# One float32 transpose, one matmul pass, in turn: re-ordering TensorE in the attention stages of a two-block transformer kernel

## The chip, the core and the metric

The kernel runs on one core of a Trainium2 chip. The metric is device time in microseconds (us) of one execution, taken as the median of several runs. TensorE is called PE in the profile; its weight loads have a row of their own (PEld) because a load can run beside the matmul before it. VectorE is DVE, ScalarE is ACT, GpSimd is POOL, and SP issues most of the DMAs.

## What is computed

Two transformer blocks on 512 tokens of width 1024, in float32. The change touches only the attention part of the first block:

```python
q = rmsnorm(q_m.reshape(bsz, s, MEM_HEADS, MEM_HEAD_DIM), memq_gain)   # 4 heads of 128
k = rmsnorm(k_m.reshape(bsz, m, MEM_HEADS, MEM_HEAD_DIM), memk_gain)   # 256 memory rows
p = softmax(q @ k.T * 128 ** -0.5);  y_mem = p @ v                     # memory attention
y_moba = moba_attention(qh, kh, vh)   # 8 heads of 64, causal over blocks of 256 keys;
                                      # with 512 tokens both blocks are always selected
merged = (sigmoid(g1 + bg1) * (y_conv @ w_br_conv) + sigmoid(g2 + bg2) * (y_moba @ w_br_moba)
          + sigmoid(g3 + bg3) * (y_mem @ w_br_mem))
```

Everything after that (the projection, two feed-forward layers, the second block) is matrix products and is not touched.

## The kernel before

**Products.** A float32 product is made of three passes over operands that were split into a high and a low part (`split`, L214 to L221): high by high, high by low, low by high. One pass is one matmul of 128 stationary by 512 moving columns. `gemm_t_steps` (L229, passes at L237 to L239) accumulates one output tile in one PSUM bank over eight k; `gemm_n_steps` (L242, passes at L249 to L251) runs four banks side by side. Both are generators: one step is three passes. `W.take` streams the weights in chunks of 128x1024: SP loads a chunk, ACT makes its high part (L96), DVE its low part (L97).

**Attention as a strand, products as filler.** `mem_head` (L521) is one head of the memory attention, `moba_pair` (L586) two heads of the block attention. Each is a strand of small PE work with long waits on ACT and DVE in between: transposes, scores, softmax, transposes of the probabilities, the product with v. `in_turns` (L265) writes a strand and, at each of its yields, as many steps of a filler as the yield says: the q, k, v projections behind the memory heads, the products of the convolution branch behind the block attention. The numbers come from `PACE_M` and `PACE_B`. Before the heads, the products for q of the memory attention (`qm_steps`) carry the transposes of k of the memory (`transpose_km`, two groups of four, both written at k = 4).

**Transposes.** A transpose is a float32 matmul of one 128x128 tile with the tile as stationary operand and an identity as moving operand, so each brings its own weight load. They come in groups of two to four into one PSUM bank. Most groups use the pool `ps_t`, which has a single bank: the next group can start only when ACT (L217) and DVE (L218) have both read the last one. In `moba_pair` the inner loop runs j = 0, 1, 2 for each of two heads: transposes (L643, L650), the split of the bank into a high part on ACT and a low part on DVE, then `PACE_B[5]` steps of filler, then the products with v (L660, L663; tile `oa`). In the first two rounds of the first head, one score product of the second head and `PACE_B[6]` steps follow the filler.

**Order.** The program order is not the order on the engines: at build time a scheduler of the framework places the instructions by its own estimate of when their inputs are ready. `as_written` (L141) takes this freedom away for the engines it names: each instruction traced inside it is tied to the one before it on its engine. In the kernel before, it holds for SP, ACT and DVE from the start to L482 and in the last stage, and nowhere for PE. Accumulating passes into one bank keep their order in any case.

Of the kernel before, what the change touches and what calls it, by code (L numbers as in the profile page):

```python
# [15 lines left out]
P = 128  # L16
S = 512
M = 256
# [12 lines left out]
FILL = (4, 8)  # L31

ORDER = (2, 3, 1, 0)

PACE_M = (5, 2, 6, 5, 5)
PACE_B = (4, 2, 2, 2, 3, 2, 1)


VECS = [
# [72 lines left out]
def build(ctx: ExitStack, tc: tile.TileContext, a: dict, out: bass.AP, dbg=None):  # L112
    nc = tc.nc
# [113 lines left out]
    def bank(p=None, tag="acc", name="acc"):  # L227
        return (p or acc).tile([P, 512], F32, tag=tag, name=name)
# [3 lines left out]
    def gemm_t_steps(ps, ops, name, row0, col):  # L232

        n = len(ops)
        for k, (ah, al) in enumerate(ops):
            wh, wl = W.take(name, row0 + k * P, col)
            mm(ps, lhsT=wh, rhs=ah, start=(k == 0), stop=False)  # L237
            mm(ps, lhsT=wh, rhs=al, start=False, stop=False)  # L238
            mm(ps, lhsT=wl, rhs=ah, start=False, stop=(k == n - 1))  # L239
            yield  # L240

    def gemm_n_steps(pss, ops, name, col):  # L242

        n = len(ops)
        for k, (ah, al) in enumerate(ops):
            wh, wl = W.take(name, k * P, col, 512)
            for i, ps in enumerate(pss):
                t = slice(i * P, (i + 1) * P)
                mm(ps, lhsT=ah[:, t], rhs=wh, start=(k == 0), stop=False)  # L249
                mm(ps, lhsT=ah[:, t], rhs=wl, start=False, stop=False)  # L250
                mm(ps, lhsT=al[:, t], rhs=wh, start=False, stop=(k == n - 1))  # L251
                yield

# [10 lines left out]
    def in_turns(strand, filler):  # L264

        for n in strand:
            for _ in range(n):
                next(filler, None)

    def rsqrt(sums, n, inv, name):  # L270

# [169 lines left out]

    pq = [bank() for _ in range(4)]
    qm_steps = gemm_n_steps(pq, h, "w_in", 3072)
    for _ in range(4):
        next(qm_steps)
    km_raw = [yp.tile([P, 512], F32, tag=f"kmr{i}", name=f"kmr{i}") for i in range(2)]
    normed_rows([(km_raw[i], pk[i]) for i in range(2)], 4, "km", rmem)
# [2 lines left out]
    nc.vector.tensor_scalar(qg[:, 1:2], V("memq_gain"), 128 ** -0.5, None, ALU.mult)  # L450
    kmT = [pair(yp, f"kmT{i}", f"kmT{i}", 1, 2 * M) for i in range(2)]

    def transpose_km():
        for g in range(2):
            pt = bank(ps_t, "pt", "kmt")
            for hh in range(2):
                for i in range(2):
                    c = (2 * g + hh) * P
                    nc.tensor.transpose(pt[:, hh * M + i * P: hh * M + (i + 1) * P], km_raw[i][:, c:c + P], ident)
            split(*kmT[g], pt, V("memk_gain"))  # L460


    for k in range(KT):
        if k == FILL[0]:
            transpose_km()
        if k >= 4:
            row_sums(ssx, k - 4)
        if k:
            for _ in range(4):
                next(qm_steps)  # L470
        if k == 0:
            for i in range(2):
                split(*vm[i], pk[2 + i], rmem[:, i:i + 1])
        elif k == 1:
            for i in range(2):
                load_rows("x", i)
        elif k == 2:
            for i in range(2, 4):
                load_rows("x", i)
        if k + 3 < KT:  # L480
            make_h(k + 3)
# [38 lines left out]

    def mem_head(hd):  # L521
        pt = bank(ps_t, "pt", "qmt")
        for i in range(4):
            nc.tensor.transpose(pt[:, i * P:(i + 1) * P], qm_raw[i][:, hd * P:(hd + 1) * P], ident)
        qT = pair(yp, "qmT", f"qmT{hd}", 1)
        split(*qT, pt, qg[:, 1:2])
        yield PACE_M[0]
# [14 lines left out]
        po = bank(ps_o, "po", "om")  # L542
        for kt in range(2):
            pt = bank(ps_t, "pt", "pmt")
            for i in range(4):
                nc.tensor.transpose(pt[:, i * P:(i + 1) * P], probs[i // 2][:, i % 2, kt * P:(kt + 1) * P], ident)
            ph, pl = pair(yp, "pmT", f"pmT{hd}_{kt}", 2)
            split(ph, pl, pt)
            yield PACE_M[3 + kt]
            vh, vl = (x[:, hd * P:(hd + 1) * P] for x in vm[kt])  # L550
            mm(po, lhsT=vh, rhs=ph, start=(kt == 0), stop=False)
            mm(po, lhsT=vh, rhs=pl, start=False, stop=False)
            mm(po, lhsT=vl, rhs=ph, start=False, stop=(kt == 1))
        split(*y_mem[hd], po)

    filler = qkv_steps()
    for _ in range(FILL[1]):
        next(filler)
    for hd in range(4):
        in_turns(mem_head(hd), filler)  # L560
# [25 lines left out]
    def moba_pair(g):  # L586

        c = slice(g * P, (g + 1) * P)
        pt = bank(name="qt")
        for i in range(4):  # L590
            nc.tensor.transpose(pt[:, i * P:(i + 1) * P], q_raw[i][:, c], ident)

        qq = [at.tile([P, S], F32R, tag=f"qq{s_}", name=f"qq{g}{s_}") for s_ in range(2)]
        for s_ in range(2):
# [2 lines left out]
            nc.vector.scalar_tensor_tensor(qq[s_][e, :], pt[d, :], qg[d, 0:1], qq[s_][d, :].bitcast(F32),  # L597
                                           op0=ALU.mult, op1=ALU.subtract)
        pt = bank(ps_s, "ps", "kt")
        for i in range(4):  # L600
            nc.tensor.transpose(pt[:, i * P:(i + 1) * P], k_raw[i][:, c], ident)
        for s_ in range(2):
            d, e = slice(64 * s_, 64 * s_ + 64), slice(64 - 64 * s_, P - 64 * s_)
            split(kk[d, s_, :], kz[d, s_, :], pt[d, :], V("moba_k_gain")[d, :])
# [31 lines left out]
        for s_ in range(2):  # L636
# [2 lines left out]
            fl = dict(skip_group_check=True)  # L639
            for j in range(3):  # L640
                pt = bank(ps_t, "pt", "pat")
                for i in range(j, 4):
                    nc.tensor.transpose(pt[:, i * P:(i + 1) * P], probs[s_][i][:, j * P:(j + 1) * P], ident)  # L643
                if j < 2:
                    c0, o = j * P, j * P
                    ph, pl = pair(at, f"pT{j}", f"pT{g}{s_}{j}", 1, S - o)
                else:
                    c0, o = P, 0
                    ph, pl = pz
                    nc.tensor.transpose(pt[:, P:2 * P], probs[s_][3][:, 3 * P:], ident)  # L650
                split(ph[:, c0 - o:], pl[:, c0 - o:], pt[:, c0:])
                yield PACE_B[5]
                if todo:
# [553 lines left out]
```

## Time and profile before

| | |
|---|---|
| median of 3 runs | 1639.43 us (1638.73 to 1639.57) |
| the profiled execution's own time | 1637.88 us |
| its span, first to last instruction | 1636.2 us |
| PE busy, share of the span | 1623.8 us, 99% |
| PE weight loads busy | 1342.2 us, 82% |
| DVE, ACT busy | 58%, 41% |
| mean granted TensorE clock | 0.999 |

The span is what the trace covers; 1.7 us lie around it. The stages that the change touches are from about 40 us (transposes of the memory's k) to about 255 us (the end of the block attention); the other 1,380 us are not touched. A busy share of 99% of PE counts a matmul from its start to its modelled end, which overlaps the next one; what one matmul costs is read from the distance between two starts.

### The profile page before, as it was taken

The page shows a single profiled execution, that of the slowest core. Times are in us where ns is not written, and L with a number is a line of the kernel's source. Part 1 is how long each engine was busy: PE and PEld are TensorE (multiplying, and loading weights), DVE is VectorE, ACT ScalarE, POOL GpSimd, SP SyncE. Part 2 cuts the span into 40 slices and gives each one's busy share as a digit, 9 for nine tenths or more (in the row PEclk, how much of TensorE's full clock was granted, in tenths as well). Part 3 has the DMA queues.
Part 4 walks back from the last instruction along what each step waited for, and adds up shares of the span by engine and source line. Part 5 has one row for each costly group of instructions (what it writes and reads, how often), then busy time and mean ns, then how long its engine had stood idle before and what let it go on. Part 6 is the DMA issues. An engine that isn't in the chain of part 4 may idle for free.

```text
span 1636.2 us, 18773 instructions
## 1 busy us (share of the span) xinstructions
PE 1623.8 (99%) x7452; PEld 1342.2 (82%) x7452; DVE 941.2 (58%) x1341; ACT 676.6 (41%) x985; POOL 24.0 (1%) x32
## 2 busy tenths in 40 slices
PE   9999999999999999999999999999999999999997
PEld 7788778888888888888888888888888888888897
DVE  6667774445567656553334943554477777753355
ACT  6657773223344333332224332333344444432252
POOL 0000000000000000000001200000000000000001
PEclk9999999999999999999999999999999999999999
DMA  8322222234333232333332323233333332333331
GB/s 327 103 78 65 65 65 91 90 112 133 103 93 101 90 103 92 102 94 99 95 125 91 99 95 103 78 95 98 101 105 100 94 99 94 102 92 103 91 116 52
DMA packets 47688, 165.02 MB, mean 101 GB/s; under 512 B 5360, under 2 KB 6768, under 8 KB 47600
## 3 DMA queue, kind: packets, MB, share of 16 engines
q1 hardware_dynamic: 46880, 163.03, 31.7%
q8 instruction: 58, 0.95, 0.2%
q10 hardware_dynamic: 720, 0.79, 0.1%
q14 instruction: 30, 0.25, 0.0%
HBM read 161.71 MB, written 2.10 MB: 100 GB/s over the span
## 4 chain that ended last, share of the span: by engine, by line
PE 96%; DVE 1%; ACT 1%; DMA 1%; issue 0%; ACTq 0%; DVEq 0%
PE acc L239 27%; PE acc L238 27%; PE acc L237 27%; PE acc L249 3%; PE acc L251 3%; PE acc L250 3%; PE oa L660 1%; DMA wraw<-in_weights 1%; PE acc L1008 0%; PE acc L1009 0%; PE acc L1010 0%; PE acc L1033 0%; PE acc L1035 0%; PE acc L1034 0%; PE pat L643 0%; PE sg L897 0%
## 5 line engine op out<-in xcount | busy, mean ns | idle before, releaser
L96 ACT ACTIVATE whi<-wraw 128x1024 fp32r<-128x1024 f32 (+1 forms) x289 | 305.2, 1057 | 565.7 <-PE acc L238 350.3
L97 DVE TENSOR_TENSOR wlo<-wraw,whi 128x1024 fp32r<-128x1024 f32 (+1 forms) x289 | 353.2, 1222 | 212.7 <-ACT whi L96 210.8
L780 ACT ACTIVATE ca<-ca 128x512 f32<-128x512 f32 x44 | 27.8, 632 | 81.2 <-DVE ca L674 81.2
L237 PE MATMUL acc<-h0h,whi 128*128 128x512 f32 x156 | 61.1, 392 | 0.0
L238 PE MATMUL acc<-h7l,whi 128*128 128x512 f32 x156 | 61.0, 391 | 0.0
L237 PE MATMUL acc<-h3h,whi 128*128 128x512 f32 x156 | 61.0, 391 | 0.0
L239 PE MATMUL acc<-h4h,wlo 128*128 128x512 f32 x156 | 61.0, 391 | 0.0
L238 PE MATMUL acc<-h5l,whi 128*128 128x512 f32 x156 | 60.9, 390 | 0.0
L237 PE MATMUL acc<-h2h,whi 128*128 128x512 f32 x156 | 60.9, 390 | 0.0
L237 PE MATMUL acc<-h6h,whi 128*128 128x512 f32 x156 | 60.9, 390 | 0.0
L239 PE MATMUL acc<-h1h,wlo 128*128 128x512 f32 x156 | 60.9, 390 | 0.0
L238 PE MATMUL acc<-h1l,whi 128*128 128x512 f32 x156 | 60.8, 390 | 0.0
L239 PE MATMUL acc<-h7h,wlo 128*128 128x512 f32 x156 | 60.8, 390 | 0.0
L238 PE MATMUL acc<-h2l,whi 128*128 128x512 f32 x156 | 60.8, 390 | 0.0
L237 PE MATMUL acc<-h1h,whi 128*128 128x512 f32 x156 | 60.8, 390 | 0.0
L238 PE MATMUL acc<-h3l,whi 128*128 128x512 f32 x156 | 60.8, 390 | 0.0
L237 PE MATMUL acc<-h7h,whi 128*128 128x512 f32 x156 | 60.8, 390 | 0.0
L239 PE MATMUL acc<-h0h,wlo 128*128 128x512 f32 x156 | 60.8, 390 | 0.0
L238 PE MATMUL acc<-h0l,whi 128*128 128x512 f32 x156 | 60.8, 390 | 0.0
L239 PE MATMUL acc<-h2h,wlo 128*128 128x512 f32 x156 | 60.7, 389 | 0.0
L237 PE MATMUL acc<-h5h,whi 128*128 128x512 f32 x156 | 60.7, 389 | 0.0
L239 PE MATMUL acc<-h5h,wlo 128*128 128x512 f32 x156 | 60.7, 389 | 0.0
(1286 smaller groups left out, 4061.0 us busy)
## 6 DMA issues: line engine op xcount, KB each, us to landing
wraw<-in_weights SPq DMA_DIRECT2D x287, 512.0 KB, 3.5
xs<-in_xT SPq DMA_DIRECT2D x4, 512.0 KB, 6.1
x<-in_x SPq DMA_DIRECT2D x4, 512.0 KB, 9.3
x<-in_xT SPq DMA_DIRECT2D x8, 256.0 KB, 4.8
out<-o SPq DMA_DIRECT2D x6, 256.0 KB, 2.1
mem<-in_mem SPq DMA_DIRECT2D x2, 512.0 KB, 6.7
memT<-in_memT SPq DMA_DIRECT2D x3, 256.0 KB, 5.3
wraw<-in_weights SPq DMA_DIRECT2D x2, 256.0 KB, 3.8
```

Of the source, the lines that this page charges most:

```text
L96: nc.scalar.activation(hi[:, s], raw[:, s], AF.Copy)
L97: nc.vector.tensor_tensor(lo[:, s], raw[:, s], hi[:, s].bitcast(F32), ALU.subtract)
L237: mm(ps, lhsT=wh, rhs=ah, start=(k == 0), stop=False)
L238: mm(ps, lhsT=wh, rhs=al, start=False, stop=False)
L239: mm(ps, lhsT=wl, rhs=ah, start=False, stop=(k == n - 1))
L249: mm(ps, lhsT=ah[:, t], rhs=wh, start=(k == 0), stop=False)
L250: mm(ps, lhsT=ah[:, t], rhs=wl, start=False, stop=False)
L251: mm(ps, lhsT=al[:, t], rhs=wh, start=False, stop=(k == n - 1))
L660: mm(po[:, c:], lhsT=vj, rhs=x[:, c - o:], start=(j == 0 and x is ph), stop=False, **fl)
L780: nc.scalar.activation(ca, ca, func)
```

## The change

Four things are done. The product generators yield after each pass and not after each three. A new generator, `woven`, issues transposes one at a time, yields 1 after each, and holds PE to program order for as long as it runs, so that transpose, pass, transpose, pass is the order on PE within one group. All seven places of the attention stages that issue transposes go through it. The pace numbers are now in passes: in a memory head 15, 6, 18, 15, 15 passes become 12, 6, 16, 10, 10 beside four woven ones for each of three groups; in the block attention 12, 6, 6, 6, 9, 6, 3 become 9, 4, 4, 4, 6, 3, 1 beside the woven ones. `transpose_km` takes a group number: one group is woven at k = 4, the other at k = 5. The number of transposes, passes, splits and DMAs is the same.

```diff
-PACE_M = (5, 2, 6, 5, 5)
-PACE_B = (4, 2, 2, 2, 3, 2, 1)
+PACE_M = (12, 6, 16, 10, 10)
+PACE_B = (9, 4, 4, 4, 6, 3, 1)
...
             mm(ps, lhsT=wh, rhs=ah, start=(k == 0), stop=False)
+            yield
             mm(ps, lhsT=wh, rhs=al, start=False, stop=False)
+            yield
             mm(ps, lhsT=wl, rhs=ah, start=False, stop=(k == n - 1))
             yield
...
+    def woven(pairs):
+        with as_written(mybir.EngineType.PE):
+            for dst, src in pairs:
+                nc.tensor.transpose(dst, src, ident)
+                yield 1
...
-    def transpose_km():
-        for g in range(2):
-            pt = bank(ps_t, "pt", "kmt")
...
+    def transpose_km(g):
+        pt = bank(ps_t, "pt", "kmt")
+        yield from woven([(pt[:, hh * M + i * P: hh * M + (i + 1) * P], km_raw[i][:, (2 * g + hh) * P:(2 * g + hh + 1) * P])
+                          for hh in range(2) for i in range(2)])
+        split(*kmT[g], pt, V("memk_gain"))
...
-        if k == FILL[0]:
-            transpose_km()
         if k >= 4:
             row_sums(ssx, k - 4)
+        done = 0
+        if 0 <= k - FILL[0] < 2:
+            for n in transpose_km(k - FILL[0]):
+                next(qm_steps)
+                done += 1
         if k:
-            for _ in range(4):
+            for _ in range(12 - done):
                 next(qm_steps)
...
-            for i in range(4):
-                nc.tensor.transpose(pt[:, i * P:(i + 1) * P], probs[i // 2][:, i % 2, kt * P:(kt + 1) * P], ident)
+            yield from woven([(pt[:, i * P:(i + 1) * P], probs[i // 2][:, i % 2, kt * P:(kt + 1) * P]) for i in range(4)])
...
-                for i in range(j, 4):
-                    nc.tensor.transpose(pt[:, i * P:(i + 1) * P], probs[s_][i][:, j * P:(j + 1) * P], ident)
+                yield from woven([(pt[:, i * P:(i + 1) * P], probs[s_][i][:, j * P:(j + 1) * P]) for i in range(j, 4)]
+                                 + [(pt[:, P:2 * P], probs[s_][3][:, 3 * P:])] * (j == 2))
```

The groups for q of a memory head (L524), and for q and k of a block-attention pair (L591, L601), are replaced in the same way.

## Rows read from the trace of the kernel before

**Rows 1.** The page: busy time, share of the span and instructions of each engine, and the chain of work that ended last, by engine.

```profile
PE 1623.8 (99%) x7452; PEld 1342.2 (82%) x7452; DVE 941.2 (58%) x1341; ACT 676.6 (41%) x985; POOL 24.0 (1%) x32
...
PE 96%; DVE 1%; ACT 1%; DMA 1%; issue 0%; ACTq 0%; DVEq 0%
```

**Rows 2.** Stretches: start and end, length, busy us and instruction count of PE, PEld, DVE, ACT, POOL, then the granted TensorE clock, the DMA share and GB/s. The first is the stage with the transposes of the memory's k, the second the memory heads, the third the block attention.

```profile
28.00:63.00 35.00, 34.48 (x154) 27.42 (x152) 26.54 (x65) 23.38 (x36) 0.00 (x0) 1.00 0.57 199
63.00:138.00 75.00, 74.94 (x374) 59.98 (x373) 46.74 (x89) 46.72 (x98) 0.00 (x0) 1.00 0.24 77
138.00:255.00 117.00, 116.35 (x584) 92.47 (x582) 91.46 (x169) 87.04 (x180) 0.00 (x0) 1.00 0.21 64
```

**Rows 3.** All transposes that the change touches, grouped by line (PE, 28 to 262 us): count, busy us, mean ns of one from start to modelled end.

```profile
L643 PE MATMUL pat<-ident,pr 128*128 128x128 f32 x72 | 11.7, 272 | 0.0
...
L546 PE MATMUL pmt<-ident,pm 128*128 128x128 f32 x32 | 5.7, 275 | 0.0
...
L601 PE MATMUL kt<-ident,k 128*128 128x128 f32 x16 | 3.1, 272 | 0.0
L524 PE MATMUL qmt<-ident,qmr 128*128 128x128 f32 x16 | 2.9, 275 | 0.1
L591 PE MATMUL qt<-ident,q 128*128 128x128 f32 x16 | 2.9, 272 | 0.0
...
L650 PE MATMUL pat<-ident,pr 128*128 128x128 f32 x8 | 2.2, 272 | 0.0
...
L459 PE MATMUL kmt<-ident,kmr 128*128 128x128 f32 x8 | 1.2, 272 | 0.0
```

**Rows 4.** Timeline of PE, an undisturbed run of passes: the first and the last of 38, 37 distances (start us, us from start to modelled end).

```profile
28.82 0.39 PE L249 MATMUL acc<-whi,h0h 128*128 128x512 f32 x1
...
37.20 0.39 PE L250 MATMUL acc<-wlo,h3h 128*128 128x512 f32 x1
```

**Rows 5.** Timeline of PE: a group of four transposes issued together (x4: one row for all four), the pass behind it and the next one.

```profile
77.19 0.60 PE L546 MATMUL pmt<-ident,pm 128*128 128x128 f32 x4
77.55 0.48 PE L249 MATMUL acc<-whi,h7h 128*128 128x512 f32 x1
77.86 0.40 PE L250 MATMUL acc<-wlo,h7h 128*128 128x512 f32 x1
```

**Rows 6.** Timeline of PE: transposes that stand alone between two passes in the kernel before. Between a transpose and the next row shown lies the start of one pass.

```profile
64.05 0.27 PE L524 MATMUL qmt<-ident,qmr 128*128 128x128 f32 x1
...
64.39 0.40 PE L249 MATMUL acc<-whi,h4h 128*128 128x512 f32 x1
...
74.58 0.27 PE L546 MATMUL pmt<-ident,pm 128*128 128x128 f32 x1
...
74.93 0.27 PE L546 MATMUL pmt<-ident,pm 128*128 128x128 f32 x1
...
75.28 0.40 PE L250 MATMUL acc<-wlo,h7h 128*128 128x512 f32 x1
75.51 0.39 PE L251 MATMUL acc<-whi,h7l 128*128 128x512 f32 x1
```

**Rows 7.** Timeline of the weight loads (PEld) of the same place: the load of the pass that follows the first and the second of the lone transposes.

```profile
74.59 0.19 PEld L251 LDWEIGHTS acc<-whi,h6l 128*128 128x128 f32 x1
...
74.93 0.19 PEld L249 LDWEIGHTS acc<-whi,h7h 128*128 128x128 f32 x1
```

**Rows 8.** Timeline of all engines in one round of the block attention's inner loop (pair 1, first head, j = 1): ACT's work on a weight chunk, the transposes, the split on ACT and DVE, the first and second product with v, and the transposes of j = 2. Rows between are left out.

```profile
184.28 1.06 ACT L96 ACTIVATE whi<-wraw 128x1024 fp32r<-128x1024 f32 x1
...
184.31 0.49 PE L643 MATMUL pat<-ident,pr 128*128 128x128 f32 x3
...
185.25 0.47 ACT L217 ACTIVATE pT101h<-pat 128x384 fp32r<-128x384 f32 x1
...
185.76 0.56 DVE L218 TENSOR_TENSOR pT101l<-pat,pT101h 128x384 fp32r<-128x384 f32 x1
185.77 0.19 PEld L660 LDWEIGHTS oa<-pT101h,v 128*128 128x128 f32 x1 [0.24 <-ACT pT101h L217]
185.80 0.41 PE L660 MATMUL oa<-pT101h,v 128*128 128x384 f32 x1
186.05 0.40 PE L238 MATMUL acc<-h1l,whi 128*128 128x512 f32 x1
...
186.52 0.34 PE L660 MATMUL oa<-pT101l,v 128*128 128x384 f32 x1
...
186.70 0.38 PE L643 MATMUL pat<-ident,pr 128*128 128x128 f32 x2
```

**Rows 9.** Waits of the weight loads in the block attention (138 to 262 us): who waited for whom, us in total, times, longest. The lines with tiles pT (pair, head, j) are eleven, one wait each; the first and the last of them are shown.

```profile
PEld oa L660 <- ACT pzh L217: 2.6, 8, 0.4
PEld sa L618 <- ACT kk L605: 1.7, 4, 0.8
...
PEld oa L660 <- ACT pT011h L217: 0.4, 1, 0.4
...
PEld oa L660 <- ACT pT100h L217: 0.2, 1, 0.2
```

**Rows 10.** Timeline of PE: the products for q of the block attention begin. One bank gets its passes for k = 0, 1, 2 before the next bank gets those for k = 0.

```profile
53.98 0.39 PE L249 MATMUL acc<-whi,h2h 128*128 128x512 f32 x1
...
54.73 0.50 PE L249 MATMUL acc<-whi,h0h 128*128 128x512 f32 x1
```

More of the change, by code (lines that the diff above doesn't have):

```diff
@@ L249, in gemm_n_steps @@
                 mm(ps, lhsT=ah[:, t], rhs=wh, start=(k == 0), stop=False)
+                yield
                 mm(ps, lhsT=ah[:, t], rhs=wl, start=False, stop=False)
+                yield
                 mm(ps, lhsT=al[:, t], rhs=wh, start=False, stop=(k == n - 1))
@@ L443, in build @@
     qm_steps = gemm_n_steps(pq, h, "w_in", 3072)
-    for _ in range(4):
+    for _ in range(12):
         next(qm_steps)
@@ L451, in build @@
     kmT = [pair(yp, f"kmT{i}", f"kmT{i}", 1, 2 * M) for i in range(2)]
-    def transpose_km():
-        for g in range(2):
-            pt = bank(ps_t, "pt", "kmt")
[L456 to L460, printed above, removed]
+    def transpose_km(g):
[3 more added lines that the diff above has]
+        split(*kmT[g], pt, V("memk_gain"))
     for k in range(KT):
-        if k == FILL[0]:
-            transpose_km()
         if k >= 4:
             row_sums(ssx, k - 4)
+        done = 0
[3 more added lines that the diff above has]
+                done += 1
         if k:
-            for _ in range(4):
+            for _ in range(12 - done):
                 next(qm_steps)
@@ L522, in mem_head @@
         pt = bank(ps_t, "pt", "qmt")
-        for i in range(4):
-            nc.tensor.transpose(pt[:, i * P:(i + 1) * P], qm_raw[i][:, hd * P:(hd + 1) * P], ident)
+        yield from woven([(pt[:, i * P:(i + 1) * P], qm_raw[i][:, hd * P:(hd + 1) * P]) for i in range(4)])
         qT = pair(yp, "qmT", f"qmT{hd}", 1)
@@ L544, in mem_head @@
             pt = bank(ps_t, "pt", "pmt")
-            for i in range(4):
-                nc.tensor.transpose(pt[:, i * P:(i + 1) * P], probs[i // 2][:, i % 2, kt * P:(kt + 1) * P], ident)
+            yield from woven([(pt[:, i * P:(i + 1) * P], probs[i // 2][:, i % 2, kt * P:(kt + 1) * P]) for i in range(4)])
             ph, pl = pair(yp, "pmT", f"pmT{hd}_{kt}", 2)
@@ L556, in build @@
     filler = qkv_steps()
-    for _ in range(FILL[1]):
+    for _ in range(3 * FILL[1]):
         next(filler)
@@ L589, in moba_pair @@
         pt = bank(name="qt")
-        for i in range(4):
-            nc.tensor.transpose(pt[:, i * P:(i + 1) * P], q_raw[i][:, c], ident)
+        yield from woven([(pt[:, i * P:(i + 1) * P], q_raw[i][:, c]) for i in range(4)])
         qq = [at.tile([P, S], F32R, tag=f"qq{s_}", name=f"qq{g}{s_}") for s_ in range(2)]
@@ L599, in moba_pair @@
         pt = bank(ps_s, "ps", "kt")
-        for i in range(4):
-            nc.tensor.transpose(pt[:, i * P:(i + 1) * P], k_raw[i][:, c], ident)
+        yield from woven([(pt[:, i * P:(i + 1) * P], k_raw[i][:, c]) for i in range(4)])
         for s_ in range(2):
@@ L649, in moba_pair @@
                     ph, pl = pz
-                    nc.tensor.transpose(pt[:, P:2 * P], probs[s_][3][:, 3 * P:], ident)
                 split(ph[:, c0 - o:], pl[:, c0 - o:], pt[:, c0:])
```

## The prediction

> **What bounds the kernel.** I read the page first: PE is busy 99% of the span and carries 96% of the chain that ended last [rows 1], so time is gained or lost only where PE's own sequence gets shorter or longer. Then the table by stretches: in the three stages that the change touches PE is never off for more than a few tenths of a microsecond, and the clock granted is 1.00, the 2.4 GHz level, in all three [rows 2]; there is no clock to win back. So busy shares say nothing more here, and I went on to the distances between starts on PE's timeline, to the weight loads, and last to the waits.
>
> The price of a pass: 37 distances from 28.82 to 37.20 us make 8.38 us, 0.227 us each [rows 4]; among the attention work it is 75.51 - 75.28 = 0.23 us [rows 6].
>
> **What the change removes, adds and moves.**
>
> *The weave.* 72 + 32 + 16 + 16 + 16 + 8 + 8 = 168 transposes are touched [rows 3]. All of them stay; what can change is what each takes on PE.
>
> In a group of four, the transposes and the pass behind them take 77.86 - 77.19 = 0.67 us [rows 5]. Less 0.23 for the pass, 0.44 us are left, 0.11 us for each transpose. That is far more than its 128 columns ask for: at the rate of a pass they would stream in 0.227 x 128 / 512 = 0.057 us. So a transpose waits for weights, and the hope behind a weave is that a pass of 0.23 us hides that load.
>
> The trace has already tried it. Some transposes stand alone between two passes in the kernel before. From the transpose to the second pass start behind it: 64.39 - 64.05 = 0.34, 74.93 - 74.58 = 0.35, 75.28 - 74.93 = 0.35 us [rows 6]. Less the pass, 0.23, each lone transpose costs 0.11 to 0.12 us: the same as in a group, or a hundredth more. The weight loads say why. The load of the pass that follows a lone transpose starts at 74.59 and at 74.93, with the transpose (74.58, 74.93) and not before it [rows 6, 7]. The pass ahead does hide the load of the transpose; but the transpose, with 0.057 us of columns, can't hide the load of the pass behind it. There is one load for every matmul in either order, and the short matmuls are short of cover by the same amount: in a group the load of the next transpose sticks out, in the weave that of the pass.
>
> So the weave is worth 168 x (0.110 - 0.11 to 0.12) = 0 to -1.7 us, that is, nothing up to a loss of 1.7. I take the mean of the three lone cases, 0.117, less 0.110, for the 160 or so that stand in groups now: 160 x 0.007 = +1.1 us.
>
> The Trainium skill ("TensorE: Matmul & The Clock Gate", section "LDWEIGHTS (loading the stationary operand)") gives a load's time as its columns over 1.2 GHz, 107 ns for 128 columns, whatever follows. The trace's 0.11 us a transpose agrees, and by that rule too the weave gains nothing.
>
> *Fewer passes between the strand's steps.* The numbers of passes and small products are the same in all; only their places change, and passes that the paces no longer place are run by a later step. In the round shown [rows 8], the transposes start at 184.31, ACT's copy ends at 185.25 + 0.47 = 185.72, DVE's at 185.76 + 0.56 = 186.32, and the next transposes start at 186.70 in the bank that DVE has read. Counting from the last of the three transposes (184.31 + 2 x 0.11 = 184.53), the first product with v follows after 1.27 us and the next group after 2.17 us. Less the last transpose and the two products with v (0.11, 0.25, 0.18 us) that is 1.63 us, seven passes' worth.
>
> The weave changes this twice. The first product with v waits for ACT in 8 + 11 = 19 of 24 rounds [rows 9]. One such wait costs PE more than the shortfall, because the load of the matmul behind it is late too: from the product at 185.80 to the pass at 186.05 it is 0.25 us where its 384 columns ask for 0.17 (0.227 x 384 / 512). With 0.05 to 0.1 us ahead of it I estimate 0.15 us a wait, 19 x 0.15 = 2.9 us in all. Behind the change one woven pass and the three of `PACE_B[5]` stand between the last transpose and this product: 0.11 + 4 x 0.23 = 1.03 us, where ACT's copy was there 185.72 - 184.53 = 1.19 us after the last transpose here, with ACT first busy on a weight chunk from 184.28 for 1.06 us [rows 8]. That is about as tight as now. It can save all 2.9 us or nothing; I take half, -1.5 us.
>
> *The single bank.* After that product, the next group must wait for DVE. What the strand has to offer in the 2.17 us is now four passes and two products, 4 x 0.23 + 2 x 0.18 = 1.28 us. The other 0.9 us must come from passes that stand further back, and the ones next in line are tied behind the waiting transposes. I cost this at nothing, because passes of another accumulation cover it; without that cover it is the loss below. That PE's order does take passes from another bank when one can't go on is seen where one bank gets k = 0, 1, 2 before the next gets k = 0 [rows 10].
>
> *The rest.* `transpose_km` moves one of two groups from k = 4 to k = 5, 12 passes or 2.7 us later. The second pass of k = 3 starts at 37.20 us [rows 4], so k = 5 begins 22 passes later, near 42 us; its result is first used by the scores of the first head, whose q is still being transposed at 64.05 us [rows 6]: 20 us of cover. In the memory heads at least ten passes, 2.3 us, stand behind each woven group: more than the 2.17 us just counted. SP's queue, the number of DMAs and the chunk sequence don't change. The end of the strand is not on the path: PE has later products to run.
>
> **Sum.** On the profiled execution's 1637.88 us (1636.2 of span and 1.7 around it): +1.1 - 1.5 = -0.4, 1637.5. The median of the runs stands 1639.43 - 1637.88 = 1.55 us above that execution, so I forecast 1639.0 us: no difference. A change under 0.2%, 3.3 us, is about what a measurement of this kernel can't tell from none.
>
> **Rivals.**
>
> *The loads do hide (faster).* If, against the lone transposes, a woven transpose cost only its columns, 0.057 us, the change would win 168 x (0.110 - 0.057) = 8.9 us: 1630.5. For it speaks only that the lone transposes are few and stand next to other small work; against it, that they agree within a hundredth and that the loads' starts give the reason. Chance 0.07. The Trainium skill, same page, section "Back-to-back issue gap", gives some 81 ns for each pair of load and 128-column matmul in a stream, with loads pulled ahead; by it the win would be 168 x 0.029 = 4.9 us, 1634.5; the rows above show 110 ns and not 81.
>
> *Waits vanish (faster).* All 2.9 us of the waits on ACT go, and part of those of the scores on `kk`, four waits of 1.7 us in all [rows 9], because q's transposes are written earlier relative to the scores. 2.9 + 1.7 - 1.1 = 3.5 us: 1635.9. It needs every wait to go; the fixed order makes new ones as easily. Chance 0.11.
>
> *The fixed order leaves PE standing (slower).* The place is the single bank in the block attention. Tied passes can't run ahead of a transpose that waits for DVE; where no other accumulation has its weights and a bank ready, PE stands for 0.9 us. Of 24 rounds, 16 have no score product in the gap: 16 x 0.9 = 14.4 us, 1639.0 + 14.4 = 1653.4. It decides from four rounds on (4 x 0.9 = 3.6 us). The same mechanism works in small: each round in which the transposes come late by a tenth, with the late load behind them, another 0.1, costs 0.2 us, 24 x 0.2 = 4.8 us, 1643.8. For it: the convolution's products use one bank at a time, so all of the next passes hang on one tied pass. Against it: eight k of the next bank have their weights, since two chunks are made ahead. Chance 0.23, most of it near the small form.
>
> *No difference* has the rest, 0.59; its own range is 1636.2 to 1642.7, from the loss of 1.7 us with new waits to most of the 2.9 us won.
>
> **The range** of 8 in 10 goes from 1634 (all waits and a little more) to 1648 (ten of the 16 rounds uncovered): it leaves out the hidden loads below and the upper part of the stalled rounds above. Faster by over 0.2%: 0.07 + 0.11 = 0.18. Slower by over 0.2%: 0.23. Within: 0.59.
>
> **What would show it.** In the profile after, a woven transpose with its pass takes 0.34 to 0.35 us from start to second start; 0.29 would mean that the loads hide. Waits of `oa` on ACT should be fewer than 19. If the single bank decides, the timeline between 138 and 255 us shows PE idle before L643, ended by DVE L218, and the stage grows. If the strand's step from group to group is covered, passes of two accumulations alternate there. I would be wrong in kind if the time moved by more than 3 us outside 40 to 260 us.

## The result, and the profile of the changed kernel

Four runs of the changed kernel have a median of 1663.25 us, against 1639.26 us for four runs of the kernel before: ratio 1.0145 [1.0132, 1.0158], 24.0 us slower. The forecast was no difference, and the time lies above the range. The profiled execution grew by 26.3 us of span (1636.2 to 1662.5).

The page of the changed kernel: busy time and instructions of each engine, and the chain that ended last, by engine.

```profile
PE 1634.4 (98%) x7452; PEld 1344.3 (81%) x7452; DVE 942.8 (57%) x1341; ACT 677.3 (41%) x985; POOL 24.4 (1%) x32
...
PE 93%; DVE 3%; ACT 3%; DMA 1%; issue 0%; ACTq 0%; DVEq 0%
```

The instruction counts are those of [rows 1]. PE's busy time rose by 10.6 us with the same work, and DVE and ACT, which had 1% of the chain each, now have 3%: PE waits for them. The page doesn't say where; the stretches do (columns as in [rows 2], and the last three rows are three short stretches inside the block attention).

```profile
28.00:63.00 35.00, 33.43 (x148) 26.33 (x147) 27.08 (x68) 23.83 (x37) 0.00 (x0) 1.00 0.57 204
63.00:138.00 75.00, 74.89 (x369) 59.30 (x369) 45.14 (x85) 45.08 (x94) 0.00 (x0) 1.00 0.25 77
138.00:255.00 117.00, 102.85 (x475) 77.11 (x474) 79.30 (x147) 74.36 (x152) 0.00 (x0) 0.93 0.16 50
157.00:160.20 3.20, 3.20 (x12) 2.30 (x11) 1.07 (x3) 2.37 (x7) 0.00 (x0) 0.53 0.00 0
187.00:190.80 3.80, 3.80 (x12) 2.87 (x13) 0.86 (x3) 2.17 (x5) 0.00 (x0) 0.51 0.21 86
223.20:228.30 5.10, 5.10 (x15) 3.79 (x15) 2.01 (x4) 3.80 (x8) 0.00 (x0) 0.50 0.01 3
```

Against [rows 2] the first two stages stand nearly as they were (PE stands for 1.57 us in the first, before for 0.52). In the third, PE is busy for 102.85 us where it was for 116.35, and issues 475 instructions where it issued 584: it stands still for 14.15 us instead of 0.65. Besides, the granted clock, 1.00 before, has a mean of 0.93: for 3.2 + 3.8 + 5.1 = 12.1 us of nearly unbroken PE work it was about 0.5, the lower level, 1.2 GHz, and so it was from 183.9 to 187.0 and from 221.5 to 223.2 us, where PE stands half of the time.

How much of the loss arises there is read from a landmark far behind it, four transposes of the second block, first row of the kernel before, second of the changed one. The third row is a wait of the changed kernel close to its end:

```profile
1571.79 0.60 PE L320 MATMUL n4p<-ident,n4s 128*128 128x128 f32 x4
```

```profile
1596.38 0.60 PE L332 MATMUL n4p<-ident,n4s 128*128 128x128 f32 x4
...
1608.61 0.38 PE L1015 MATMUL acc<-h0h,whi 128*128 128x256 f32 x1 [1.73 <-ACT pwr L996]
```

The landmark comes 24.6 us later. From 300 us on PE has no wait ahead of it in either kernel, so these 24.6 us are lost before. The other 1.7 us of the span are the wait of the third row. It lies far from the change, and nothing here shows that the change causes it: among the versions below e8 has it with 1.5 us and e17 with 0.2. The 24.6 us are made of 14.15 - 0.65 = 13.5 us of PE standing in the block attention, 1.05 us more of it in the first stage, some 12.1 x (1 - 0.51) = 5.9 us of half clock, and about 4 us left over for the rest of the half clock and for what I read as late loads and short waits, a share that I didn't measure by itself.

What PE waits for (PE, 28 to 300 us; total us, times, longest), in the kernel before and then in the changed one:

```profile
PE acc L251 <- DVE h3l L221: 0.5, 1, 0.5
PE sa L618 <- ACT kk L605: 0.4, 1, 0.4
```

```profile
PE sa L626 <- ACT pr L506: 7.6, 5, 2.7
PE qt L279 <- ACT pr L506: 1.5, 2, 0.8
PE sa L626 <- ACT kk L613: 1.5, 3, 0.7
PE oa L667 <- DVE pT101l L218: 1.4, 1, 1.4
PE acc L255 <- DVE h3l L221: 1.2, 1, 1.2
PE pat L279 <- ACT pr L509: 0.9, 1, 0.9
PE kt L279 <- ACT pr L506: 0.8, 1, 0.8
...
```

ACT's L506 is the exponential of the softmax, which reads the scores out of their bank, and L509 scales the probabilities. Most of the listed wait is for the softmax, by score products (sa, L626) and transposes (L279); the kernel before had to wait for the softmax at the same places, but its list has none of this, because PE had passes to run (its weight loads for scores waited for it four times, 0.5 us at the longest). One such place on PE's timeline, in the kernel before (start, us to modelled end; between the first two rows shown stand nine more passes, all of them 0.23 us apart):

```profile
149.65 0.40 PE L238 MATMUL acc<-h5l,whi 128*128 128x512 f32 x1
...
151.95 0.39 PE L239 MATMUL acc<-h0h,wlo 128*128 128x512 f32 x1
152.18 0.50 PE L618 MATMUL sa<-kk,qq 128*128 128x512 f32 x1
```

and in the changed kernel:

```profile
151.20 0.39 PE L626 MATMUL sa<-kk,qq 128*128 128x256 f32 x1 [0.50 <-ACT pr L506]
...
151.78 0.48 PE L237 MATMUL acc<-h0h,whi 128*128 128x512 f32 x1
152.10 0.39 PE L239 MATMUL acc<-h0l,whi 128*128 128x512 f32 x1
152.33 0.40 PE L241 MATMUL acc<-h0h,wlo 128*128 128x512 f32 x1
154.31 0.51 PE L626 MATMUL sa<-kk,qq 128*128 128x512 f32 x1 [1.58 <-ACT pr L506]
...
155.80 0.33 PE L279 MATMUL qt<-ident,q 128*128 128x128 f32 x1 [0.76 <-ACT pr L506]
155.88 0.48 PE L237 MATMUL acc<-h1h,whi 128*128 128x512 f32 x1
...
157.77 0.41 PE L279 MATMUL pat<-ident,pr 128*128 128x128 f32 x1
157.83 0.78 PE L241 MATMUL acc<-h3h,wlo 128*128 128x512 f32 x1
158.41 0.41 PE L279 MATMUL pat<-ident,pr 128*128 128x128 f32 x1
```

Before, eleven passes fill the time up to the next score product (2.53 us). After, three do; then PE stands for 1.58 us, and for 0.76 us more. The next pass of that accumulation is h1h of 155.88, and it is written behind the first transpose of the next group for q, which itself waits for a bank that L506 frees. From there on transpose and pass take 158.41 - 157.77 = 0.64 us together; at full clock, later in this stage, four pairs, from the first transpose to the pass behind the fourth pair, take 199.84 - 198.47 = 1.37 us, 0.343 each:

```profile
198.47 0.27 PE L279 MATMUL pat<-ident,pr 128*128 128x128 f32 x1
...
199.84 0.40 PE L237 MATMUL acc<-h5h,whi 128*128 128x512 f32 x1
```

### The profile page after: what moved, and what is told of

It reads as the page before. It is cut to its first block, busy times and chain, and to the rows that moved or that the text cites. A ratio compares the mean times of both kernels' runs of the same rounds, so it can differ in the third digit from the quotient of the medians.

```text
span 1662.5 us, 18782 instructions
## 1 busy us (share of the span) xinstructions
PE 1634.4 (98%) x7452; PEld 1344.3 (81%) x7452; DVE 942.8 (57%) x1341; ACT 677.3 (41%) x985; POOL 24.4 (1%) x32
## 4 chain that ended last, share of the span: by engine, by line
PE 93%; DVE 3%; ACT 3%; DMA 1%; issue 0%; ACTq 0%; DVEq 0%
PE acc L241 26%; PE acc L239 26%; PE acc L237 26%; PE acc L251 2%; PE acc L255 2%; PE acc L253 2%; DMA wraw<-in_weights 1%; PE oa L667 1%; PE pat L279 1%; ACT whi L96 1%; ACT pr L506 0%; PE acc L1015 0%; PE acc L1040 0%; PE acc L1042 0%; PE acc L1041 0%
## 5 line engine op out<-in xcount | busy, mean ns | idle before, releaser
L241 PE MATMUL acc<-h6h,wlo 128*128 128x512 f32 x156 | 61.7, 395 | 0.0
L239 PE MATMUL acc<-h6l,whi 128*128 128x512 f32 x156 | 61.6, 395 | 0.0
L241 PE MATMUL acc<-h3h,wlo 128*128 128x512 f32 x156 | 61.6, 395 | 0.0
L237 PE MATMUL acc<-h4h,whi 128*128 128x512 f32 x156 | 61.5, 394 | 0.0
L239 PE MATMUL acc<-h4l,whi 128*128 128x512 f32 x156 | 61.5, 394 | 0.0
```

## The experiments

Theory T: the time is lost because passes are held behind transposes that have to wait. Rivals: the weave itself costs PE time; the new paces place too few passes; the order among the transposes matters; the weight chunks run out. The edits are to the changed kernel unless another is named, each ratio is to runs of the kernel before that were taken beside it, with a 95% interval, and the two numbers of microseconds are the medians, the kernel before second. A line "..." stands for lines of an edit that are left out.

**The order alone, the paces alone.**

```diff
 # e1_untied: in woven
-        with as_written(mybir.EngineType.PE):
-            for dst, src in pairs:
...
+        for dst, src in pairs:
...
 # e2_long_pace: the order stays
-PACE_B = (9, 4, 4, 4, 6, 3, 1)
+PACE_B = (12, 6, 6, 6, 9, 6, 3)
 # e3_batched: in woven, no order, transposes together, passes behind
+        for dst, src in pairs:
+            nc.tensor.transpose(dst, src, ident)
+        for _ in pairs:
+            yield 1
 # e4_heads_only: the block attention as before: all its groups by a plain loop, together()
+PACE_B = (12, 6, 6, 6, 9, 6, 3)
-        yield from woven([(pt[:, i * P:(i + 1) * P], q_raw[i][:, c]) for i in range(4)])
+        yield from together([(pt[:, i * P:(i + 1) * P], q_raw[i][:, c]) for i in range(4)])
...
```

> The changed kernel with the fixed order on PE left out; yields, paces and the one-by-one writing of the transposes stay. Theory A (the tie is the cost: a pass that is tied behind a waiting transpose takes the whole accumulation behind it out of play, so PE has no passes left while the softmax holds the banks): the waits of the scores on ACT (7.6 us) shrink to under 2 us, no stretch falls to the 1.2 GHz level, 1638 to 1643 us. Theory B (the shorter paces are the cost: too few passes are written between the scores): about as the changed kernel, 1655 to 1664 us. A mix lies between.

> The changed kernel, woven and tied, but the paces of the block attention as long as they were before, in passes: 12, 6, 6, 6, 9, 6, 3. Theory A (the tie): PE still stands where the tied passes hang on transposes, the longer paces give some of it back, 1650 to 1660 us. Theory B (the shorter paces): the loss is gone, 1638 to 1643 us.

> The changed kernel with the transposes of a group written together and free, the passes that stood between them written behind the group; paces as in the changed kernel. Theory A (the tie): 1638 to 1643 us. Theory B (the shorter paces): 1655 to 1664 us. Against the untied kernel of the same call it shows what writing them one by one is worth: by the lone transposes of the kernel before, 0 to 1.7 us in favour of this one.

> Weave and tie in the transposes of the memory's k and in the memory heads only; the block attention as before, paces in passes of the same length. Both theories that place the loss in the block attention: 1638 to 1643 us. If the memory heads carry part of it: above 1645 us.

- e1: 1639.96 against 1639.30 us, 1.0006 [0.9996, 1.0015]. Without the fixed order no loss can be measured.
- e2: 1654.54 against 1639.30, 1.0094 [1.0079, 1.0109]. With the paces of before beside the woven passes 15 us are still lost; but see e8 and e11: these paces use up the filling passes early.
- e3: 1638.62 against 1639.30, 0.9994 [0.9985, 1.0004]. The new paces alone, the small half of the change, do nothing that can be measured. Against e1, which writes the same transposes one by one, it is 1.34 us ahead, inside the 0 to 1.7 us that were expected of it.
- e4: 1640.45 against 1639.30, 1.0006 [0.9997, 1.0016]. Woven and tied in the memory's k and the memory heads, the change costs nothing there that can be measured, 2.6 us at most by the interval: the loss is in the block attention, as the profile said.

The stretch of the block attention in e1, to be read against [rows 2] and the third row above, and its waits on PE:

```profile
138.00:255.00 117.00, 115.62 (x583) 91.54 (x582) 93.19 (x173) 88.99 (x184) 0.00 (x0) 1.00 0.20 64
```

```profile
PE sa L625 <- ACT kk L612: 1.3, 3, 0.5
```

The line is the longest of PE's waits there. The clock is 1.00 again without the standing of PE, and no wait of PE on the softmax is left.

**Which order, and of which groups.** e5_tie_transposes holds only each transpose behind the one before it; e6_tie_qk holds to program order only the groups for q and k in the block attention (and the heads), e7_tie_probs only those of the probabilities (and the heads). e8_batched_more is e3 with more passes.

```diff
 # e5_tie_transposes, in woven
+                if last is not None:
+                    tc.add_manual_dep(i, last.name, mybir.DependencyInfo(
+                        mybir.DependencyClass.NoSync, mybir.DependencyReason.DATA), reason="order")
 # e6_tie_qk (untied() is woven() without as_written)
-                yield from woven([(pt[:, i * P:(i + 1) * P], probs[s_][i][:, j * P:(j + 1) * P]) for i in range(j, 4)]
+                yield from untied([(pt[:, i * P:(i + 1) * P], probs[s_][i][:, j * P:(j + 1) * P]) for i in range(j, 4)]
 # e7_tie_probs: the groups for q and for k
-        yield from woven([(pt[:, i * P:(i + 1) * P], q_raw[i][:, c]) for i in range(4)])
+        yield from untied([(pt[:, i * P:(i + 1) * P], q_raw[i][:, c]) for i in range(4)])
...
 # e8_batched_more: e3, and
+PACE_B = (9, 4, 4, 4, 6, 6, 3)
```

> The changed kernel with the transposes of a group tied to each other in their order, but the passes between them free. If the cost is that passes are tied (an accumulation out of play behind a waiting transpose): as the untied kernel, 1638 to 1642 us. If the cost is the fixed order of the transposes themselves (one that is ready must wait for one that is not): above 1645 us.

> Weave everywhere, but in the block attention only the groups for q and k are tied; those of the probabilities are free. The timeline of the changed kernel shows two open accumulations at a standstill, one behind a transpose of the probabilities that waits for the softmax, one behind a transpose of the next pair's q that waits for a bank. If both ties are needed for PE to stand (one accumulation left free covers the wait): under 1645 us here and in the twin run. If the ties of q and k carry the loss: above 1652 us. If the losses add up, this and the twin run together lose 23 us against the untied one.

> The twin: in the block attention only the groups of the probabilities are tied, those for q and k are free. If both ties are needed: under 1645 us. If the ties of the probabilities carry the loss: above 1652 us. If the losses add up: the rest of 23 us.

> A try for a version that beats both: transposes of a group together and free, and three passes more behind each group of the probabilities and two more behind the two score products (paces 9, 4, 4, 4, 6, 6, 3). If the first product with v then no longer waits for ACT, up to 3 us less than the kernel before, 1636 us; if the scheduler moves the passes anyway, no difference, 1638 to 1641 us.

- e5: 1639.77 against 1639.10, 1.0004 [0.9995, 1.0014]: the order among transposes costs nothing that can be measured.
- e6: 1639.63, 1.0002 [0.9993, 1.0011]; e7: 1652.26, 1.0073 [1.0056, 1.0090], 13.2 us. The probability groups carry the loss. The two don't add up: the ties for q and k cost nothing alone and 24.0 - 13.2 = 11 us on top of the others.
- e8: 1651.76, 1.0070 [1.0055, 1.0085], a miss: more passes among the groups were no gain but a loss of 12.7 us, with nothing tied. By the code a pair now takes 97 passes; three take 291, and the convolution has 288, so the fourth pair has none written beside it. The trace agrees: DVE reads the convolution's last product at 236.4 us, and the first transpose of the fourth pair runs at 236.2 (kernel before: 235.7 and 219.8).

e7, PE's timeline in the second pair: after a score product PE stands for 3.27 us before a transpose that waits for the scaled probabilities (L515 here), and the passes come back only behind it, at the lower level of the clock (0.78 us):

```profile
178.78 0.40 PE L633 MATMUL sa<-kz,qq 128*128 128x512 f32 x1
182.45 0.48 PE L279 MATMUL pat<-ident,pr 128*128 128x128 f32 x1 [3.27 <-ACT pr L515]
182.58 0.78 PE L241 MATMUL acc<-h4h,wlo 128*128 128x512 f32 x1
```

e8, in the fourth pair, the longest of its waits for `kk`, which come to 7.7 us in all:

```profile
241.86 0.69 PE L626 MATMUL sa<-kk,qq 128*128 128x384 f32 x1 [4.26 <-ACT kk L613]
```

**The price of a weave by itself.** On the kernel before, 576 transposes whose result nobody reads are added to the gate products, behind the attention and its waits, in fixed order: in e9 four behind every fourth pass, in e10 one behind each.

```diff
+            spare = bank(ps_t, "pt", "spare")
+            with as_written(mybir.EngineType.PE):
...
                         done += 1
+                        for q in range(0 if done % 4 else 4):      # e9_spare_grouped
+                            nc.tensor.transpose(spare[:, q * P:(q + 1) * P], mask, ident)
+                        q = (done - 1) % 4                         # e10_spare_woven
+                        nc.tensor.transpose(spare[:, q * P:(q + 1) * P], mask, ident)
 # e11_batched_long: e3, and
+PACE_B = (12, 6, 6, 6, 9, 6, 3)
```

> The kernel before, with 576 transposes more that nobody reads: 24 in each of the 24 gate products of the first block, behind the attention, where nothing has to wait; four together behind every fourth pass, PE in fixed order there. At 0.11 us each, as in the groups of the kernel before: 63 us more, 1702 us. The twin run puts one behind each pass.

> The same 576 spare transposes, one behind each pass of the gate products, in fixed order. If a lone transpose costs its load as in a group (0.110 to 0.117 us): as the twin run or up to 4 us longer, 1702 to 1707 us. If the pass hides the load, so that a transpose costs its columns alone (0.057 us): 31 us less than the twin, about 1671 us.

> Transposes together and free, paces 12, 6, 6, 6, 9, 6, 3 and the passes of the groups on top, as in the tied kernel with the long paces. One pair then writes 109 passes, so that the convolution's 288 are used up before the fourth pair begins. If the loss of the kernel with 97 passes a pair (12 us) came from a fourth pair without written passes: above 1648 us here too, and the tied kernel with long paces (1654.5 us) owes most of its loss to that. If it came from something else in that kernel: 1638 to 1643 us.

e9 took 1711.59 us, 1.0445 [1.0427, 1.0462], and e10 1712.40, 1.0448 [1.0433, 1.0464] (kernel before 1638.58): 0.81 / 576 = 1.4 ns more for each woven transpose, which is not told from nothing, since e10's four runs alone spread over 4.0 us. In the profile of e9 four transposes and four passes take 332.61 - 331.24 = 1.37 us:

```profile
331.24 0.60 PE L707 MATMUL spare<-ident,mask 128*128 128x128 f32 x4
...
332.61 0.60 PE L707 MATMUL spare<-ident,mask 128*128 128x128 f32 x4
```

and in e10, woven, 332.37 - 331.00 = 1.37 us:

```profile
331.00 0.27 PE L707 MATMUL spare<-ident,mask 128*128 128x128 f32 x1
331.02 0.48 PE L704 MATMUL acc<-h3h,whi 128*128 128x512 f32 x1
...
332.37 0.27 PE L707 MATMUL spare<-ident,mask 128*128 128x128 f32 x1
```

Between passes a transpose costs what it costs in a group, and the weight loads of e10 show it as [rows 7] do, the load of a pass starting with the transpose ahead of it (331.34 us on PE as well):

```profile
331.34 0.19 PEld L704 LDWEIGHTS acc<-h3l,whi 128*128 128x128 f32 x1
```

The price is (1.37 - 4 x 0.227) / 4 = 0.115 us in place; the whole program grew by 73.0 / 576 = 0.127 us for each, the rest of it at the end of the block attention. There the gate products, now in fixed order, fill less: 8 of their passes run before the last product with v in e9 and 2 in e10, where 38 did in the kernel before, and PE stands for 3.1 us (e10: 3.5) between 138 and 255 us, at a mean clock of 0.98. Behind it the fixed order costs nothing: from 320 to 600 us of e10, where no transpose has to wait, PE is busy for 280.00 of 280 us at a clock of 1.00. e11 took 1645.23 us, 1.0038 [1.0024, 1.0051]: I expected more than 1648. Its convolution is used up early as well (last product read at 227.9 us, the fourth pair's first transpose at 227.8). Writing too many passes early costs 6.6 us here without any tie, so part of e2's 15 us may be that and not the order. Why e8 with fewer passes costs twice as much stays open; PE's waits for `kk` are 7.7 us there and 0.3 us in e11.

**Chunks, and a second accumulation.** If a tied pass holds its accumulation, it holds its weight chunk too. e13 adds a fourth chunk buffer for a quarter of chunks 26 to 35; e12 is its control, with the room for it taken from the memory heads' results in both: two of the four heads overwrite the other two, whose results are left out.

```diff
 # e12_three_chunks, e13_four_chunks
-    y_mem = [pair(ymem_pool, f"ym{i}", f"ym{i}", 1) for i in range(4)]
+    y_mem = [pair(ymem_pool, f"ym{i}", f"ym{i}", 1) for i in range(2)] * 2
 # e13_four_chunks
+            if self.spare is not None and 26 <= c < 36 and c % 4 == 3:
+                hi = self.spare.tile([P, CW], F32R, tag="whx", name=f"whi{c}", bufs=1)
 # e14_two_fillers: tied passes from one half of the convolution, the paces from the other
+    free, tied = conv_steps((0, 1)), conv_steps((2, 3))
 # e15_two_fillers_untied: e14 without as_written
 # e16_own_chunks: e14, each accumulation with a chunk of its own
+        hi, lo = W.whole(name, col)
```

> Control for the twin run: the changed kernel, but the third and fourth memory head write over the first and second one's result, which frees SBUF (that part of the output is the wrong one). Under every theory the time of the changed kernel, 1660 to 1666 us.

> The same with a fourth buffer for split weight chunks during the block attention (the freed SBUF holds it; results of the memory heads overwritten as in the control). One accumulation of the convolution uses one chunk, and a chunk stays held until its last pass is run. If PE runs dry because a tied pass holds its chunk, so that only two more accumulations, 48 passes, can be run around it: one more accumulation, 24 passes or 5.5 us, covers most of the waits, under 1651 us. If PSUM banks or the scheduler's own estimates set the limit: as the control, above 1656 us.

> The changed kernel, tied as it is, but the filler of the block attention in two: the passes tied between the transposes come from the products of the third and fourth channel group of the convolution, the paced passes, never tied, from those of the first and second. So an accumulation that no transpose holds is open nearly all the time. If a tied pass costs because it takes the only open accumulation out of play: most of the loss is gone, under 1650 us. If PE stands for another reason (banks, or the scheduler's own estimates of when a transpose is ready): above 1655 us.

> Control: the two fillers without the tie in the block attention (the memory heads stay woven and tied). If two fillers cost nothing by themselves: 1638 to 1643 us. What this one is longer than that is the price of two open accumulations, to be taken off the twin run.

> The tied kernel with two fillers again, but each accumulation takes a weight chunk of its own, where before the pieces of both fillers alternated in one chunk, so that a tied pass held the chunk of the free filler too (the trace shows a free pass waiting for DVE's L97, and that for a tied pass). If PE stands in the changed kernel because every accumulation of the filler has a tied pass after at most three free ones: free passes now cover the waits, under 1650 us. If banks or the scheduler's estimates of when a transpose is ready are the cause: above 1655 us, as with shared chunks.

- e12: 1662.55 against 1639.66, 1.0140 [1.0125, 1.0155]; e13: 1663.56, 1.0144 [1.0127, 1.0161]. A fourth buffer for a quarter of these chunks changes nothing, so the chunk buffers are not the limit as far as this one tests it.
- e14: 1675.27 against 1639.34, 1.0217 [1.0200, 1.0234], and its control e15 1639.43, 1.0001 [0.9992, 1.0011]. With the ties in one half alone the loss is larger. But the two halves shared weight chunks, so free passes could wait for tied ones (next two fences of e14: DVE's step of a chunk waits for a pass, and a free pass for DVE).

```profile
158.84 1.22 DVE L97 TENSOR_TENSOR wlo<-wraw,whi 128x1024 fp32r<-128x1024 f32 x1 [0.75 <-PE acc L241]
```

```profile
160.12 0.50 PE L241 MATMUL acc<-h7h,wlo 128*128 128x512 f32 x1 [0.28 <-DVE wlo L97]
```

- e16: 1669.38 against 1638.94, 1.0185 [1.0168, 1.0202]. With chunks of their own, 30 us are still lost, so my theory that one accumulation without ties covers the waits falls. Its rows: the low half of the last chunk made before it is ready at 156.87 + 1.22 = 158.09 us and the next chunk is only begun at 168.82, so the next free accumulation has its weights from 158.09 on at the latest. Yet its first pass runs at 169.34, right behind the first transpose for q of the next pair. Whether the banks' order or the order that the scheduler chose for PE kept it there, these runs don't tell apart.

```profile
156.87 1.22 DVE L97 TENSOR_TENSOR wlo<-wraw,whi 128x1024 fp32r<-128x1024 f32 x1
```

```profile
169.32 0.27 PE L310 MATMUL qt<-ident,q 128*128 128x128 f32 x1
169.34 0.48 PE L261 MATMUL acc<-h0h,whi 128*128 128x512 f32 x1
```

**Each half of the order.** The order that `woven` sets has two kinds of links: a pass held behind the transpose ahead of it (e17), and a transpose held behind the pass ahead of it (e18).

```diff
 # e17_pass_behind
+                    if last is not None and last.name in turned and i.name not in turned:
+                        tc.add_manual_dep(i, last.name, mybir.DependencyInfo(
+                            mybir.DependencyClass.NoSync, mybir.DependencyReason.DATA), reason="order")
 # e18_transpose_behind
+                    if last is not None and last.name not in turned and i.name in turned:
+                        tc.add_manual_dep(i, last.name, mybir.DependencyInfo(
+                            mybir.DependencyClass.NoSync, mybir.DependencyReason.DATA), reason="order")
```

> The tie cut in half: each pass is held behind the transpose written ahead of it, but no transpose is held behind a pass. If the loss comes from products waiting for a transpose, and with it for the softmax: most of the 24 us, above 1652 us. If it comes from transposes held back behind passes: 1638 to 1643 us.

> The other half: each transpose is held behind the pass written ahead of it, but no pass behind a transpose. If products waiting for a transpose are the cause: 1638 to 1643 us. If transposes held back behind passes are the cause: above 1652 us. If only the full chain does it: both runs under 1645 us.

e17: 1658.38 against 1639.39, 1.0112 [1.0097, 1.0127], 19 us. e18: 1639.98, 1.0005 [0.9995, 1.0015]. The stretch of the block attention, e17 and then e18:

```profile
138.00:255.00 117.00, 105.98 (x496) 80.53 (x495) 81.22 (x155) 78.43 (x166) 0.00 (x0) 0.94 0.16 50
```

```profile
138.00:255.00 117.00, 115.63 (x582) 91.50 (x581) 92.78 (x172) 88.99 (x184) 0.00 (x0) 1.00 0.20 64
```

and the longest line of PE's waits in e17, which e18 doesn't have:

```profile
PE sa L642 <- ACT pr L522: 4.9, 3, 2.8
```

This bears T out: the link that costs by itself is the pass behind the transpose. It brings back 19 of the 24 us with PE standing for 117 - 105.98 = 11.0 us and a mean clock of 0.94; the other link costs nothing alone. What the two cost together beyond that, 5 us, I can't place.

No version beat the kernel before: e3 is 0.7 us ahead, within its interval.

## Why the prediction was wrong

**The step that failed** is "The single bank", and in it one sentence: "I cost this at nothing, because passes of another accumulation cover it". They didn't. The evidence for it, one bank's passes among another's [rows 10], comes from a stage in which nothing was tied. There I asked whether PE takes passes out of order; the question was whether what remains free behind a tied pass is ready, and in e16, where the weights were ready, it still didn't run. The stated objection, that "all of the next passes hang on one tied pass", was the true one, and I weighed it at 0.23. In place of nothing the runs show 14.15 us of PE standing in 117 (before: 0.65), and 19 us lost by this link alone (e17).

**The rival "The fixed order leaves PE standing"** is what happened, with another place and a higher price. I put it before the transposes, which wait for DVE's reading of the single bank in the inner rounds, 16 times 0.9 us. The wait there hardly shows: DVE's L218 ends 1.4 us of the waits listed for PE, and that before a product with v. PE stands in the softmax of the scores instead, 7.6 us before L626 alone, because a score product needs a bank and a transpose needs probabilities that ACT hasn't finished, up to 2.7 us at once (3.27 in e7). I looked at one inner round [rows 8] and never at the stretch from a score product to the next, where the kernel before runs eleven passes in one wait. The price lacked a part as well: the clock, which I had read as having nothing to give [rows 2], fell after PE stood, some 5.9 us or a little more. So 24.0 us, where the rival had 14.4 and the range ended at ten rounds of it, 1648.

**The weave** was right. A woven transpose with its pass takes 0.343 us, inside the 0.34 to 0.35 that I named, and e9 and e10 give the same time for either order. The cost of +1.1 us for 160 transposes comes to 160 x 0.0014 = 0.2 us by their difference and to 1.34 us by e1 against e3, where 71 of e1's 168 transposes still stand directly before another; the size of this term stays open at about 0 to 1.3 us. The prediction set 0.11 us beside the time of a load; that was a distance between transposes, and the rows of the loads last longer, 0.19 us for a pass [rows 7]. "The loads do hide" is refuted: at 0.053 us each, 576 transposes would have brought 31 us between the twins. The 81 ns that the Trainium skill ("TensorE: Matmul & The Clock Gate", section "Back-to-back issue gap") gives for a load and a 128-column matmul is not met here, at 110 to 115 ns.

**The waits on ACT** were right in direction; what they are worth isn't shown. Products with v that wait for ACT fell from 19 to 10 (three for pzh, and seven lines of pT), but those on DVE's half rose from 4 to 12, two lines of which are these (weight loads, 138 to 285 us):

```profile
PEld oa L667 <- DVE pT101l L218: 1.8, 1, 1.8
PEld oa L667 <- DVE pzl L218: 1.1, 4, 0.4
...
PEld oa L667 <- ACT pzh L217: 0.8, 3, 0.3
```

In a kernel with so much standing this says little of the term. e3, without ties, is the cleaner case: there the waits on ACT fell to 12, and the time by 0.7 us, which its interval doesn't tell from nothing. The term of -1.5 us is neither shown nor refuted.

**The rest.** The stages ahead of 138 us cost nothing, as costed (e4). The paces were nothing too (e3), but not for every pace: e8 and e11 point to a limit that the prediction didn't look at, that the passes written beside the pairs are a stock, 288, that must last into the fourth pair; by the code the changed kernel takes 75 a pair and the kernel before 81, so that both run out only within the fourth. Two small sums are off and change nothing: k = 5 begins at 44.6 us in the changed kernel and not near 42, which still leaves most of the 20 us of cover, and the faster rivals are counted from the median of 1639.4, the slower one from the forecast of 1639.0.

## What to carry to other kernels

Work that fills another chain's waits should not be ordered behind an instruction of that chain: one link from a waiting transpose to a filling pass holds all the filling that hangs on the pass (19 us in e17), and a busy share of 99% doesn't show how many waits are being filled. The other direction, the chain held behind the filling, cost nothing here (e18), and filling that is written out beside a chain must not be used up too early (e8, e11). A short matmul with a weight load of its own gained nothing from a long neighbour (1.37 us for four of each, in either order): the load of the long one then starts late instead.

## What the runs showed of the hardware that was not expected

The granted clock fell in a stage that had been at 1.00 throughout: in the profile above PE had stood for 0.50, 1.58 and 0.76 us between 150.7 and 155.8 us, and from 157.0 to 160.2 us the granted clock was 0.53; passes were 0.64 us apart together with their transpose, against 0.343 at the full level. Where PE hardly stood, woven transposes left it at 1.00 (e10 from 320 to 600 us; e1 and e18, in part woven, from 138 to 255). Not every wait brought it down: PE also stood for 0.73 us before 250.74 and for 1.67 us before 253.72, and from 249 to 262 us the clock stayed at 1.00. So a wait can cost more than its own length: 12.1 us of half clock, some 5.9 us, came with 13.5 us of standing.
